# Sliding-window attention in a decoder layer: turned probabilities leave PSUM by a plain ScalarE copy, and the masked ones meet the difference of two neighbouring blocks' values

## The chip, the core and the metric

The kernel runs on one core of a Trainium2 chip. The metric is the device time of one execution in microseconds (us); the time before is 1079.05 us, the median of three runs from 1078.88 to 1079.31 us. The engines are named as in the profile: PE is TensorE (PEld its weight loads), ACT is ScalarE, DVE is VectorE, POOL is GpSimd, and SP issues most of the DMAs. A row of the trace gives the start in us from the beginning of the span, then the length, the engine, the source line, the operation and the tiles with their shapes.

## The reference, cut to what matters

One decoder layer is computed for 1024 prompt tokens and 8 x 4 sample tokens. Half of its mixing part is grouped-query attention with 8 query heads and 2 key/value heads of 64 elements, where each query sees itself and the 127 keys before it:

```python
d = a + WINDOW - c                       # query a of a block, key c of (block before, own block)
mask = (d >= 0)[None] & (d < WINDOW)[None] & (blk * WINDOW + c[None] - WINDOW >= 0)
...
m = jnp.maximum(jnp.max(s, axis=-1, keepdims=True), sink)
p = jnp.exp(s - m)
denom = jnp.sum(p, axis=-1, keepdims=True) + jnp.exp(sink - m)
w = (p / denom).astype(v.dtype)
return jnp.einsum('bnhgqk,bnkhd->bnqhgd', w, v)
```

A query at place a of a block (of 128 tokens) sees exactly 128 keys: those at places 0 to a of its own block and those at places a+1 to 127 of the block before. So one tile of 128 x 128 per head holds all its scores: column k belongs to the own block where k <= a and to the block before where k > a.

## The kernel before, in words

Features lie on the partitions and tokens on the free axis; the 1056 tokens are three groups of 352. All large products run on PE as three matmuls on split operands (high times high, high times low, low times high), 128x352 each. The program has one stage after another: the input projections (to about 129 us of the span), the attention (about 129 to 215 us) with the first output projections woven into it, and then the feed-forward and the per-layer input, which take the rest. `pinned` (from L572 on) keeps every instruction of PE in the order in which the program writes it. On the other engines a scheduler places the instructions, unless `tc.keep_in_program_order` (in `fix`, when `fixed[0]` is set, or directly) holds one to the written order; each engine then works through its list strictly in order.

The attention handles the eight blocks of 128 prompt tokens in the order 6, 7, 5, 0, 1, 2, 3, 4. `scores(b)` makes the scores of a block in PSUM; ACT copies four pieces of 128x256 out (L775), and DVE overwrites the columns that belong to the other half's keys (`copy_predicated`, L779). For block 0 DVE adds a mask instead (L781). `weigh(t)` is the softmax, once for each key/value head with 4 query heads: DVE takes the maximum (L721), the shift `nmx` (L723) and the sink's part `es` (L725); ACT does the exponentials (L729 for the sink, four at L732 with their sums); DVE adds and inverts the sums (L737, L738); POOL multiplies the tile by them (L740). `turned(b, t)` turns the eight 128x128 tiles on PE (L122), four into a PSUM bank; DVE takes them out twice, each time with a mask: `ptc` (L800) for the keys of the own block and `ptp` (L802) for the keys of the block before. `values(b, parts)` multiplies them by the values: in each half of the queries, `vmix` or `vtok` by `ptc`, and onto it the block before's `vtok` by `ptp`; `put` (L711 on ACT, L712 on DVE) stores the result split as high and low in `mixa`, which the output projection reads.

`filler(n)` puts n pieces of the output projection on PE between these steps: `out_pool` (12 matmuls; ACT copies the result out, L893), `out_attn` (12 matmuls that read `mixa`; DVE adds, L912, ACT squares and scales, L899, L902, L914) and `out_proj` (24 matmuls; ACT scales and squares, L922, L902). Weights come by SP's DMAs and are split by a cast of ACT (L173) and a subtraction of DVE (L174).

On PE the loop at L960 to L972 runs, for a block a and the next block b: scores(b), filler, the turning of a, filler, values(a). The first pass has no scores, since block 7's were made ahead.

Of the kernel before, what the change touches and what calls it, by code (L numbers as in the profile page):

```python
# [62 lines left out]
def trunk_kernel(  # L63
# [48 lines left out]
    def act_tile(shape, dt=F32, s="a"):  # L112
        return apool.tile(shape, dt, tag="a", bufs=A_SLOTS, name=nm(s))
# [18 lines left out]
    def bank():  # L132
        return psum.tile([P, 512], F32, tag="b", name=nm("b"))
# [33 lines left out]
    def fix(ins):  # L167

        if fixed[0]:
            tc.keep_in_program_order(ins)  # L170
# [493 lines left out]
    nc.scalar.dma_start(ps_o, pso)  # L664


    misc = act_tile([P, 6, P])
    qd, am, vdec = misc[:, 0, :], misc[:, 1:5, :], misc[: NDEC * DSEQ, 5, :]
    for c in range(4):
        ge.tensor_copy(  # L670
            qd.rearrange("p (g c e) -> p g c e", g=4, c=4)[:, :, c, :],
# [6 lines left out]
    ge.tensor_scalar(nskd, skd, -1.0, None, op0=ALU.mult)  # L678


    vtok, vmix = act_tile([P, NB, P]), act_tile([P, NB, P])

    def v_turned():
        for h in range(2):
            ps = bank()
            for i in range(4):
                b = 4 * h + i
                mt(ps[:, i * P : (i + 1) * P], vT[:, b * P : (b + 1) * P])
            v = ps.rearrange("p (b c) -> p b c", c=P)
            se.copy(vtok[:, 4 * h : 4 * h + 4, :], v)  # L690
            ge.tensor_copy(vmix[0:64, 4 * h : 4 * h + 4, :], vtok[0:64, 4 * h : 4 * h + 4, :])
        ge.tensor_copy(vmix[64:P, 1:NB, :], vtok[64:P, 0 : NB - 1, :])
        ps = bank()
        mt(ps[: NDEC * DSEQ, :P], vT[:, SEQ:])
        se.copy(vdec, ps[: NDEC * DSEQ, :P])
        nc.scalar.dma_start(kp_o, kT[:, SEQ - WIN : SEQ])
        nc.scalar.dma_start(vp_o, vtok[:, NB - 1, :])
# [17 lines left out]
    def softmax(*parts):  # L715

        scale = 0.125
        held = []
        for t, nh, sk, nsk in parts:
            mx = spool.tile([P, nh], F32, tag="mx", name=nm("mx"))  # L720
            fix(ve.tensor_reduce(mx, t, axis=AX.X, op=ALU.max))  # L721
            nmx = spool.tile([P, nh], F32, tag="nmx", name=nm("nmx"))
            fix(ve.scalar_tensor_tensor(nmx, mx, -scale, nsk, op0=ALU.mult, op1=ALU.min))  # L723
            es = spool.tile([P, nh], F32, tag="es", name=nm("es"))
            fix(ve.tensor_tensor(es, sk, nmx, op=ALU.add))  # L725
            held.append((nmx, es))
        sums = []
        for (t, nh, _, _), (nmx, es) in zip(parts, held):
            se.activation(es, es, AF.Exp)  # L729
            sm = spool.tile([P, nh], F32, tag="sm", name=nm("sm"))  # L730
            for c in range(nh):
                se.activation(  # L732
                    t[:, c, :], t[:, c, :], AF.Exp, bias=nmx[:, c : c + 1], scale=scale, accum_out=sm[:, c : c + 1]
                )
            sums.append(sm)
        for (t, nh, _, _), (_, es), sm in zip(parts, held, sums):
            fix(ve.tensor_tensor(sm, sm, es, op=ALU.add))  # L737
            fix(ve.reciprocal(sm, sm))  # L738
            nk = t.shape[2]
            ge.tensor_tensor(t, t, sm.unsqueeze(2).to_broadcast([P, nh, nk]), op=ALU.mult)  # L740
# [50 lines left out]
    def turned(b, t):  # L791

        ptc = act_tile([P, 8, WIN])
        ptp = act_tile([P, 8, WIN]) if b else None
        for kv in range(2):
            ps = bank()
            hs = slice(4 * kv, 4 * kv + 4)
            for c in range(4):
                mt(ps[:, c * P : (c + 1) * P], t[:, 4 * kv + c, :])
            fix(ve.tensor_tensor(ptc[:, hs, :], v4(ps), m4(2), op=ALU.mult))  # L800
            if b:
                fix(ve.tensor_tensor(ptp[:, hs, :], v4(ps), m4(3), op=ALU.mult))  # L802
        return ptc, ptp

    def values(b, parts):


        ptc, ptp = parts
        sides = [(kv, slice(64 * kv, 64 * kv + 64), slice(4 * kv, 4 * kv + 4)) for kv in range(2)]
        if not b:  # L810
            o = bank()
            for kv, cols, hs in sides:
                mm(o[cols, :], vtok[:, b, cols], ptc[:, hs, :], start=True, stop=True)
            put(o, 0, WIN)
            return
        q = [slice(0, 64), slice(64, P)]
        os_ = [bank() for _ in range(2)]
        for i, v in enumerate((vmix, vtok)):
            for kv, cols, hs in sides:
                mm(os_[i][cols, :256], v[:, b, cols], ptc[:, hs, q[i]], start=True, stop=False)  # L820
        for i in range(2):
            for kv, cols, hs in sides:
                mm(os_[i][cols, :256], vtok[q[i], b - 1, cols], ptp[q[i], hs, q[i]], start=False, stop=True)
        for i in range(2):
            put(os_[i], b * WIN + 64 * i, 64)

# [133 lines left out]
    for a, b in zip(order, order[1:] + [None]):  # L960

        fixed[0] = lazy[0] = b is None
        t2 = ahead or (None if b is None else scores(b))
        ahead = None
        filler(1)
        parts = turned(a, t)
        if b is None:
            lazy[0] = False
            weights(WOA[1][0], 1)
        filler(1)  # L970
        values(a, parts)
        t = t2  # L972
# [489 lines left out]
def _layout(i):  # L1462

    f = lambda a: np.asarray(a, dtype=np.float32) if not isinstance(a, np.ndarray) else a
    i = {k: f(v) for k, v in i.items()}
    tok = lambda a, s, c: np.concatenate([a.reshape(-1, c), s.reshape(-1, c)]).reshape(T, c // P, P).transpose(2, 1, 0)
    heads = np.concatenate([np.r_[64 * c : 64 * c + 64, 64 * (4 + c) : 64 * (4 + c) + 64] for c in range(4)])
    w_in = i["w_in"][0]
    w_in = w_in[:, np.r_[512:768, heads, 768:1280]]
    w_out = i["w_out"][0][np.r_[heads, 512:1024]]  # L1470
    tiles = lambda w: w.reshape(w.shape[0] // P, P, w.shape[1] // P, P).transpose(2, 1, 0, 3)
    wd = i["w_down"][0]
    gains = np.stack([i[n][0].reshape(KC, P).T for n in ("norm_mix_pre", "norm_mix_post", "norm_ffn_pre", "norm_ffn_post")], 1)
    sinks = i["attn_sinks"][0]
    q, c = np.arange(WIN)[:, None], np.arange(WIN)[None, :]
    masks = np.stack([1.0 * np.where(q < 64, c <= q, c > q), np.where(c <= q, 0.0, NEG), 1.0 * ((q <= c) | ((q >= 64) & (c < 64))), 1.0 * (q > c)], 1)
    r = np.arange(P)[:, None]
    ri, rj = (r % 8) // DSEQ, r % DSEQ
    rb = 2 * (r // 32) + ri
    ki, kw = np.arange(2 * WIN)[None, :] // WIN, np.arange(2 * WIN)[None, :] % WIN  # L1480
    nb, nj = np.arange(NDEC * DSEQ)[None, :] // DSEQ, np.arange(NDEC * DSEQ)[None, :] % DSEQ
    dmask = np.concatenate([(ri == ki) & (kw > rj), (rb == nb) & (nj <= rj)], 1)
    pfix = np.stack([np.maximum(w / (np.arange(16) + 1.0), 1.0) for w in PW])
    out = {
        "x": tok(i["x_prompt"], i["x_sample"], D),
        "p": tok(i["p_prompt"], i["p_sample"], PLE),
        "w_in": tiles(w_in),
        "w_out_a": w_out[:, :512].reshape(2, 4, P, 2, 256).transpose(0, 3, 2, 1, 4),
        "w_out_b": tiles(w_out[:, 512:]),
        "w_pool": i["w_pool"][0].transpose(1, 0, 2),  # L1490
        "w_gu": np.stack([tiles(i["w_gate"][0]), tiles(i["w_up"][0])], 1),
        "w_dn": wd[: SLAB * NSLAB * P].reshape(NSLAB, SLAB, P, 2, 2, 2, P).transpose(0, 4, 3, 2, 1, 5, 6).reshape(NSLAB, 2, 2, P, KC, P),
        "w_dl": wd[SLAB * NSLAB * P :].reshape(REST, P, 2, 512).transpose(2, 1, 0, 3),
        "w_pg": tiles(i["w_ple_gate"][0]),
        "w_ple": i["w_ple"][0].reshape(2, P, 4, 256).transpose(2, 1, 0, 3),
        "gains": gains,
        "pscale": i["pool_scale"][0].reshape(4, P).T,
        "sink_p": np.broadcast_to(sinks, (P, 8)),
        "sink_d": np.tile(np.repeat(sinks.reshape(2, 4).T, 8, axis=0), (4, 1)),
        "masks": masks.astype(np.float32),  # L1500
        "dmask": np.where(dmask, 0.0, NEG).astype(np.float32),
        "pfix": np.broadcast_to(pfix, (P, 4, 16)).astype(np.float32),
        "ck": i["cache_k"][0].reshape(NDEC, WIN, P).transpose(2, 0, 1),
        "cv": i["cache_v"][0].reshape(NDEC, WIN, P).transpose(1, 0, 2),
        "st": i["state_pool"][0].reshape(NDEC, PST, 4, P).transpose(3, 2, 0, 1),
    }
    return {k: np.ascontiguousarray(v) for k, v in out.items()}
# [29 lines left out]
```

## Time and profile before

| what | value |
| --- | --- |
| median of the runs (three) | 1079.05 us |
| the profiled execution's own time | 1080.58 us |
| its span, first to last instruction | 1078.8 us |
| PE busy | 1069.6 us, 99% |
| DVE busy | 874.7 us, 81% |
| ACT busy | 510.2 us, 47% |
| POOL busy | 281.3 us, 26% |
| mean granted clock of TensorE | 0.998 |

Durations below are those of the profiled execution. PE's rows overlap, since matmuls are pipelined: two 128x352 matmuls in a row begin about 0.16 us apart though each row is 0.32 us long. On ACT and DVE a row begins about 0.1 us before the row ahead of it ends when nothing is waited for.

### The profile page before, as it was taken

The page shows a single profiled execution, that of the slowest core. Times are in us where ns is not written, and L with a number is a line of the kernel's source. Part 1 is how long each engine was busy: PE and PEld are TensorE (multiplying, and loading weights), DVE is VectorE, ACT ScalarE, POOL GpSimd, SP SyncE. Part 2 cuts the span into 40 slices and gives each one's busy share as a digit, 9 for nine tenths or more (in the row PEclk, how much of TensorE's full clock was granted, in tenths as well). Part 3 has the DMA queues.
Part 4 walks back from the last instruction along what each step waited for, and adds up shares of the span by engine and source line. Part 5 has one row for each costly group of instructions (what it writes and reads, how often), then busy time and mean ns, then how long its engine had stood idle before and what let it go on. Part 6 is the DMA issues. An engine that isn't in the chain of part 4 may idle for free. (4 is left out here: it accounts for less than half of the span.)

```text
span 1078.8 us, 18189 instructions
## 1 busy us (share of the span) xinstructions
PE 1069.6 (99%) x7107; PEld 1053.0 (98%) x7107; DVE 874.7 (81%) x1303; ACT 510.2 (47%) x872; POOL 281.3 (26%) x211
## 2 busy tenths in 40 slices
PE   8999999999999999999999999999999999999998
PEld 8999988899999999999999999999999999999998
DVE  6876378886979957796598898898899998969983
ACT  7423277664555533445543343344344455545431
POOL 0063032200000023454454454444442000023200
PEclk9999999999999999999999999999999999999999
DMA  8121311544543432412212212213235556464361
GB/s 299 57 74 39 102 58 37 201 159 144 201 168 131 137 98 78 152 60 93 84 60 98 79 59 98 80 59 106 73 112 182 186 160 244 152 214 162 98 201 60
DMA packets 43575, 130.91 MB, mean 121 GB/s; under 512 B 5061, under 2 KB 15717, under 8 KB 43489
## 3 DMA queue, kind: packets, MB, share of 16 engines
q1 hardware_dynamic: 42160, 127.98, 35.0%
q10 hardware_dynamic: 1328, 1.77, 0.5%
q8 instruction: 56, 0.92, 0.4%
q14 instruction: 31, 0.25, 0.1%
HBM read 113.86 MB, written 15.87 MB: 120 GB/s over the span
## 5 line engine op out<-in xcount | busy, mean ns | idle before, releaser
L1108 POOL TENSOR_TENSOR wr<-wr,wr 128x512 f32<-128x512 f32 x108 | 174.9, 1634 | 476.8 <-DMA wr<-in_w_gu_dram 238.1
L173 ACT CAST wh<-wr 128x1024 fp32r<-128x1024 f32 (+1 forms) x138 | 142.1, 1031 | 162.8 <-PE b L128 98.7
L174 DVE TENSOR_TENSOR wl<-wr,wh 128x1024 fp32r<-128x1024 f32 (+1 forms) x138 | 171.0, 1241 | 42.0 <-ACT wh L173 26.3
L128 PE MATMUL b<-fh,wh 128*128 128x352 f32 x624 | 201.7, 323 | 0.8 <-DVE p L1135 0.8
L128 PE MATMUL b<-fh,wl 128*128 128x352 f32 x624 | 200.1, 321 | 0.0
L128 PE MATMUL b<-fl,wh 128*128 128x352 f32 x624 | 200.0, 320 | 0.0
L173 ACT CAST sh<-wr 128x1024 fp32r<-128x1024 f32 x72 | 75.7, 1052 | 141.3 <-POOL wr L1108 138.9
L128 PE MATMUL b<-fh,sh 128*128 128x352 f32 x416 | 134.3, 323 | 0.0
L128 PE MATMUL b<-fl,sh 128*128 128x352 f32 x416 | 133.2, 320 | 0.0
L128 PE MATMUL b<-fh,sl 128*128 128x352 f32 x416 | 133.2, 320 | 0.0
L174 DVE TENSOR_TENSOR sl<-wr,sh 128x1024 fp32r<-128x1024 f32 x72 | 97.4, 1353 | 37.4 <-ACT sh L173 24.5
L128 PEld LDWEIGHTS b<-fh,wh 128*128 128x128 f32 x624 | 117.0, 187 | 1.5 <-DVE p L1135 1.1
L128 PEld LDWEIGHTS b<-fl,wh 128*128 128x128 f32 x624 | 117.5, 188 | 0.0
L128 PEld LDWEIGHTS b<-fh,wl 128*128 128x128 f32 x624 | 116.9, 187 | 0.0
L128 PE MATMUL b<-h,wh 128*128 128x352 f32 x480 | 105.9, 326 | 1.2 <-ACT h L449 1.1
L128 PE MATMUL b<-hid,wh 128*128 128x352 f32 x416 | 99.6, 322 | 0.0
L128 PEld LDWEIGHTS b<-h,wh 128*128 128x128 f32 x480 | 82.4, 190 | 2.5 <-ACT h L449 1.2
L1108 POOL TENSOR_TENSOR wr<-wr 128x512 f32<-128x512 f32 x36 | 50.9, 1414 | 106.7 <-DVE w L174 106.7
L128 PEld LDWEIGHTS b<-fl,sh 128*128 128x128 f32 x416 | 78.2, 188 | 0.0
L128 PEld LDWEIGHTS b<-fh,sh 128*128 128x128 f32 x416 | 78.0, 187 | 0.1
L128 PEld LDWEIGHTS b<-fh,sl 128*128 128x128 f32 x416 | 77.9, 187 | 0.0
L128 PE MATMUL b<-hp,sh 128*128 128x352 f32 x320 | 76.6, 322 | 0.9 <-DVE ap L1278 0.9
(202 smaller groups left out, 2220.7 us busy)
## 6 DMA issues: line engine op xcount, KB each, us to landing
wr<-in_w_gu_dram SPq DMA_DIRECT2D x88, 512.0 KB, 3.3
wr<-in_w_dn_dram SPq DMA_DIRECT2D x40, 512.0 KB, 3.3
wr<-in_w_pg_dram SPq DMA_DIRECT2D x16, 512.0 KB, 3.6
x<-in_x_dram SPq DMA_DIRECT2D x6, 704.0 KB, 8.6
x1d<-x SPq DMA_DIRECT2D x6, 704.0 KB, 3.6
x<-x1d SPq DMA_DIRECT2D x6, 704.0 KB, 5.1
out_y_dram<-yo SPq DMA_DIRECT2D x24, 176.0 KB, 2.3
wr<-in_w_out_b_dram SPq DMA_DIRECT2D x8, 512.0 KB, 3.3
```

The costliest lines, as they stand in the source:

```text
L128: ins = te.matmul(*args, **kw)
L173: fix(se.copy(hi, src))
L174: fix(ve.tensor_tensor(lo, src, hi.bitcast(F32), op=ALU.subtract))
L1108: ge.tensor_tensor(out, a, b, op=op)
```

## The change

The masked copy `ptc` becomes an unmasked one. On the 64 keys where a half of the queries meets both blocks, with p the turned probabilities, M their part that belongs to the block before, and v and v' the values of the own block and of the block before, the product was (p - M) v + M v', and is now p v + M (v' - v). So ACT copies the whole turned bank out, DVE makes only the masked `ptp`, and `ptp` meets `vdif`, the difference of two neighbouring blocks' values, which POOL makes once. The mask of the own block is gone from the tensor `masks` (four tiles before, three now). Two things move with it: the exponentials and the new copies on ACT are held in the written order, and the softmax of the next block is now written behind the turning of the present one.

```diff
-    misc = act_tile([P, 6, P])
-    qd, am, vdec = misc[:, 0, :], misc[:, 1:5, :], misc[: NDEC * DSEQ, 5, :]
+    misc = act_tile([P, 5, P])
+    qd, am, vdec = misc[:, 0, :], misc[:, 1:4, :], misc[: NDEC * DSEQ, 4, :]
...
-    vtok, vmix = act_tile([P, NB, P]), act_tile([P, NB, P])
+    vtok, vmix, vdif = (act_tile([P, NB, P]) for _ in range(3))
...
         ge.tensor_copy(vmix[64:P, 1:NB, :], vtok[64:P, 0 : NB - 1, :])
+        ge.tensor_tensor(vdif[:, 1:NB, :], vtok[:, 0 : NB - 1, :], vtok[:, 1:NB, :], op=ALU.subtract)
...
             for c in range(nh):
-                se.activation(
-                    t[:, c, :], t[:, c, :], AF.Exp, bias=nmx[:, c : c + 1], scale=scale, accum_out=sm[:, c : c + 1]
+                tc.keep_in_program_order(
+                    se.activation(
+                        t[:, c, :], t[:, c, :], AF.Exp, bias=nmx[:, c : c + 1], scale=scale, accum_out=sm[:, c : c + 1]
+                    )
                 )
...
-            fix(ve.tensor_tensor(ptc[:, hs, :], v4(ps), m4(2), op=ALU.mult))
+            tc.keep_in_program_order(se.copy(ptc[:, hs, :], v4(ps)))
             if b:
-                fix(ve.tensor_tensor(ptp[:, hs, :], v4(ps), m4(3), op=ALU.mult))
+                fix(ve.tensor_tensor(ptp[:, hs, :], v4(ps), m4(2), op=ALU.mult))
...
-                mm(os_[i][cols, :256], vtok[q[i], b - 1, cols], ptp[q[i], hs, q[i]], start=False, stop=True)
+                mm(os_[i][cols, :256], vdif[q[i], b, cols], ptp[q[i], hs, q[i]], start=False, stop=True)
...
-        t2 = ahead or (None if b is None else scores(b))
-        ahead = None
+        t2 = ahead or (None if b is None else scores(b, False))
         filler(1)
         parts = turned(a, t)
+        if t2 and not ahead:
+            weigh(t2)
+        ahead = None
```

The lines of the changed kernel lie a little lower: the new copy is L803 and the remaining masked product L805; L732 is L734 there, L729 is L730, L723 and L725 are L724 and L726, L711 and L712 are L712 and L713, L893 is L896, L902, L914 and L922 are L905, L917 and L925, L775 and L779 are L778 and L782, and `vdif` is L693. The order of PE's instructions is the same in both; what moves stands on ACT and DVE, at three places.

The first place is ACT's list around the values of block 6, the first block. Here `a_1497` (before) and `a_1499` (now) is the tile of block 7, whose scores were made ahead, `y` is the result of a piece of the output projection, and `a_1608` is the `ptc` of block 6. Before:

```order
L711 CAST mh_1582<-b_1427 128x4x32
L732 ACTIVATE a_1497,sm_1541<-a_1497,nmx_1536 128x128
L729 ACTIVATE es_1538<-es_1538 128x4
L732 ACTIVATE a_1497,sm_1541<-a_1497,nmx_1536 128x128 x3
L729 ACTIVATE es_1553<-es_1553 128x4
L732 ACTIVATE a_1497,sm_1556<-a_1497,nmx_1551 128x128 x4
L957 DMA out_ks_dram<-a_1586 128x1024
L893 COPY y_1285<-b_1592 128x352
```

And now:

```order
L712 CAST mh_1584<-b_1429 128x4x32
L896 COPY y_1285<-b_1594 128x352
L730 ACTIVATE es_1540<-es_1540 128x4
L734 ACTIVATE a_1499,sm_1543<-a_1499,nmx_1538 128x128 x4
L730 ACTIVATE es_1555<-es_1555 128x4
L734 ACTIVATE a_1499,sm_1558<-a_1499,nmx_1553 128x128 x4
L960 DMA out_ks_dram<-a_1588 128x1024
L803 COPY a_1608<-b_1610 128x512
L803 COPY a_1608<-b_1617 128x512
```

The copy of `y`, which waits for a filler on PE, stood behind the eight exponentials of block 7 and stands ahead of them now, and the two copies that the values of block 6 need stand behind all of these.

The second place is DVE's list where block 0's scores (`a_1775`, now `a_1777`) meet block 5's turned tiles. The waits are printed with the rows of the change. Before:

```order
L723 SCALAR_TENSOR_TENSOR nmx_1790<-mx_1788,c_1289 128x4
L723 SCALAR_TENSOR_TENSOR nmx_1805<-mx_1803,c_1289 128x4
L800 TENSOR_TENSOR a_1832<-b_1834,a_1280 128x512
L725 TENSOR_TENSOR es_1792<-c_75,nmx_1790 128x4
L725 TENSOR_TENSOR es_1807<-c_75,nmx_1805 128x4
```

And now:

```order
L805 TENSOR_TENSOR a_1805<-b_1806,a_1280 128x512 [waits Activation_49]
L805 TENSOR_TENSOR a_1805<-b_1813,a_1280 128x512 [waits Activation_49]
L726 TENSOR_TENSOR es_1824<-c_75,nmx_1822 128x4 [waits DVE_49]
L724 SCALAR_TENSOR_TENSOR nmx_1837<-mx_1835,c_1289 128x4
L726 TENSOR_TENSOR es_1839<-c_75,nmx_1837 128x4 [waits DVE_49]
```

Both masked products now stand ahead of `es`, and each waits for ACT, that is for the copy out of the same bank. On ACT the sink's exponential, which reads `es`, now comes ahead of the four others of its head, where one to three of them came first before.

The third place is ACT's list in one of the later rounds of the loop, from block 3's scores (`a_2173`, now `a_2175`) to its exponentials; `a_2236` is the `ptc` of block 2, and `sq` and `y` belong to the fillers. Before:

```order
L775 COPY a_2173<-b_2175 128x256
L775 COPY a_2173<-b_2177 128x256
L732 ACTIVATE a_2173,sm_2217<-a_2173,nmx_2212 128x128 x2
L729 ACTIVATE es_2214<-es_2214 128x4
L732 ACTIVATE a_2173,sm_2217<-a_2173,nmx_2212 128x128 x2
L729 ACTIVATE es_2229<-es_2229 128x4
L732 ACTIVATE a_2173,sm_2232<-a_2173,nmx_2227 128x128 x4
L902 ACTIVATE sq_2260<-y_1287 128x352
L914 ACTIVATE y_1287<-y_1287,c_72 128x352
```

And now:

```order
L173 CAST wh_2282<-wr_2216 128x1024
L778 COPY a_2175<-b_2177 128x256
L778 COPY a_2175<-b_2179 128x256
L905 ACTIVATE sq_2232<-y_1287 128x352
L917 ACTIVATE y_1287<-y_1287,c_72 128x352
L803 COPY a_2236<-b_2238 128x512
L803 COPY a_2236<-b_2245 128x512
L730 ACTIVATE es_2256<-es_2256 128x4
L734 ACTIVATE a_2175,sm_2259<-a_2175,nmx_2254 128x128 x4
L730 ACTIVATE es_2271<-es_2271 128x4
L734 ACTIVATE a_2175,sm_2274<-a_2175,nmx_2269 128x128 x4
```

The exponentials stood right behind the copies of the scores; now the square and the scaling of a filler's result and the two new copies stand between, and a weight cast has come in among the copies of the scores.

More of the change, by code (lines that the diff above doesn't have):

```diff
@@ L1475, in _layout @@
     q, c = np.arange(WIN)[:, None], np.arange(WIN)[None, :]
-    masks = np.stack([1.0 * np.where(q < 64, c <= q, c > q), np.where(c <= q, 0.0, NEG), 1.0 * ((q <= c) | ((q >= 64) & (c < 64))), 1.0 * (q > c)], 1)
+    masks = np.stack([1.0 * np.where(q < 64, c <= q, c > q), np.where(c <= q, 0.0, NEG), 1.0 * (q > c)], 1)
     r = np.arange(P)[:, None]
```

## The prediction

> **What bounds the kernel now.** I read the page's busy times first, then what PE waited for, then the attention by stretches, and then the rows around three places of the loop. The page's first part gives busy time, share and instructions by engine:
>
> ```profile
> PE 1069.6 (99%) x7107; PEld 1053.0 (98%) x7107; DVE 874.7 (81%) x1303; ACT 510.2 (47%) x872; POOL 281.3 (26%) x211
> ```
>
> PE is busy for 99% of the span, so only its waits can be won, and every new wait is lost in full. The list of waits of PE (line, releaser, us in total, times, longest) has one entry that this change touches:
>
> ```profile
> PE b L128 <- DVE a L800: 0.5, 1, 0.5
> ```
>
> It is the wait for a masked copy that the change removes, 0.5 us. PE's order and work don't change, so about 0.5 us bounds the gain; 0.2% of this kernel, about what a measurement can tell from no change, is 2.2 us. The stretches of the attention's later rounds (PE, PEld, DVE, ACT, POOL busy, clock, DMA):
>
> ```profile
> 180.00:190.90 10.90, 10.90 (x117) 9.94 (x116) 10.74 (x24) 8.78 (x31) 2.34 (x2) 1.00 0.29 98
> 190.90:200.00 9.10, 8.57 (x98) 6.99 (x95) 8.07 (x24) 5.53 (x24) 2.20 (x2) 1.00 0.19 60
> ```
>
> ACT is no spare engine here: of 10.9 us in the first it is busy for 8.78.
>
> **What is removed and added.** The groups (count, then busy time and mean ns) over the attention:
>
> ```profile
> L800 DVE TENSOR_TENSOR a<-b,a 128x512 f32<-128x512 f32 x16 | 10.9, 682 | 1.6 <-PE b L122 1.5
> L802 DVE TENSOR_TENSOR a<-b,a 128x512 f32<-128x512 f32 x14 | 9.4, 675 | 0.0
> L893 ACT COPY y<-b 128x352 f32<-128x352 f32 x12 | 5.2, 442 | 5.3 <-PE b L128 5.2
> L690 ACT COPY a<-b 128x512 f32<-128x512 f32 x2 | 1.1, 588 | 7.3 <-PE b L122 7.3
> ```
>
> DVE loses the 16 of L800, 10.9 us. ACT gains 16 copies of the kind of L690, 16 x 0.59 = 9.4 us, two for each block. The 14 of L802 stay, but each now waits for the copy out of its bank. `vdif` is one POOL product of 128x896; by L740's row of 128x576 below (1.15 us) it takes about 1.15 x 896/576 = 1.8 us, and it fits in POOL's idle time between these two rows, from 132.2 to 135.5:
>
> ```profile
> 131.29 0.93 POOL L692 COPY a<-a 64x896 f32<-64x896 f32 x1
> 135.53 1.15 POOL L740 TENSOR_TENSOR a<-a,sm 128x576 f32<-128x576 f32 x1 [3.31 <-ACT a L775]
> ```
>
> It and the smaller mask cost nothing there; without that cover they would delay block 6's softmax, which has until 147.74. What counts is the order on ACT: 9.4 us more of work that waits for PE's turning, with exponentials, casts and PSUM copies queued behind it. The softmax that is written later takes its maxima, its exponentials, its sums and POOL's two products with it, so PE's next turning gets them later. Three places follow; primes mark times on before's clock, without the waits added earlier.
>
> **First place, the values of block 6: +1.9 us.** The rows of PE and ACT (start, length):
>
> ```profile
> 147.58 0.32 PE L128 MATMUL b<-mh,wl 128*128 128x352 f32 x1
> 147.74 1.04 PE L122 MATMUL b<-c,a 128*128 128x128 f32 x8
> ...
> 150.61 3.01 PE L128 MATMUL b<-a,a 128*64 128x256 f32 x64
> ```
>
> ```profile
> 146.95 0.40 ACT L732 ACTIVATE a<-a,nmx 128x128 f32<-128x128 f32 x1 [0.87 <-DVE nmx L723]
> ...
> 150.24 0.94 ACT L893 COPY y<-b 128x352 f32<-128x352 f32 x2
> ```
>
> Before, block 7's exponentials ran from 146.95 to 150.24, 3.29 us, beside the filler, and `y` was copied behind them. Now `y` comes first. Its filler's last matmul ends at 147.9 (147.58 + 0.32); the copy takes 0.44, and the exponentials begin at 148.3 and end their turn at 151.6. Only then come the copies of block 6: 0.59, and 1.1 for both, so they end at 152.2 and 152.7. PE wants the first at 150.61: it waits 1.6 us there, then 0.2 for the second, since a first product of 0.26 us lies between, and at most 0.1 for the products of DVE (0.68 behind each copy). Sum 1.9. From below: 1.2, if `y` and the exponentials run somewhat closer than the rows; from above 2.3, if each of the four hand-overs costs 0.1 more.
>
> **Second place, the filler that reads block 5's result: +1.4 us.** The rows on DVE, ACT and PE:
>
> ```profile
> 160.28 1.00 DVE L737 TENSOR_TENSOR sm<-sm,es 128x4 f32<-128x4 f32 x1
> 161.31 0.18 DVE L738 RECIPROCAL sm<-sm 128x4 f32<-128x4 f32 x1
> 161.41 0.72 DVE L712 TENSOR_TENSOR ml<-b,mh 128x256 fp32r<-128x256 f32 x2
> 162.05 1.28 DVE L781 TENSOR_TENSOR a<-b,a 128x512 f32<-128x512 f32 x2
> 163.25 1.27 DVE L721 TENSOR_REDUCE mx<-a 128x4 f32<-128x512 f32 x2
> 164.43 0.28 DVE L723 SCALAR_TENSOR_TENSOR nmx<-mx,c 128x4 f32<-128x4 f32 x2
> ```
>
> ```profile
> 155.61 1.05 ACT L173 CAST wh<-wr 128x1024 fp32r<-128x1024 f32 x1 [1.29 <-PE b L128]
> ...
> 164.67 0.40 ACT L732 ACTIVATE a<-a,nmx 128x128 f32<-128x128 f32 x1 [0.84 <-DVE nmx L723]
> ...
> 167.96 0.43 ACT L893 COPY y<-b 128x352 f32<-128x352 f32 x1
> 168.44 0.65 ACT L711 CAST mh<-b 128x256 fp32r<-128x256 f32 x2
> ```
>
> ```profile
> 169.65 0.43 PE L128 MATMUL b<-mh,wh 128*128 128x352 f32 x1
> ```
>
> Before, `put` ended on ACT at 169.09 (168.44 + 0.65) and the filler began at 169.65: next to no slack. Now block 5's exponentials follow the cast, `y` and the copies of block 7: 156.6 + 0.4 + 1.0 = 158.0', and end at 161.3'. Their sum and its inverse then end at about 161.7', where they ended at 161.5 before (161.31 + 0.18), since the sum's row was held for 1.00 us. With `put` behind `y`, block 0's scores follow at 162.6' instead of 162.05: +0.5. The two maxima and `nmx` move with them, and then both L805 stand ahead of `es`: 2 x 0.64 + 0.15 (as long as one `nmx`), so ACT begins at 166.5' where it began at 164.67: +1.8. Exponentials (3.29), `y` (0.4) and both casts (0.65) end at 170.8', 1.1 us after 169.65; the low part on DVE, half of 0.72, adds 0.3. Sum 1.4. Its ends are 0, if the scheduler's rows overlap as well as before, and 2.0, if the new sum is held on DVE as the old one was, for 1.00 us.
>
> **Third place, the rounds of blocks 2 to 4: +2.6 us.** PE's values begin here:
>
> ```profile
> 185.93 3.01 PE L128 MATMUL b<-a,a 128*64 128x256 f32 x64
> ...
> 195.98 0.65 PE L128 MATMUL b<-a,a 128*64 128x256 f32 x2
> 197.11 3.01 PE L128 MATMUL b<-a,a 128*64 128x256 f32 x62 [0.48 <-DVE a L800]
> ...
> 206.88 1.68 PE L128 MATMUL b<-a,a 128*64 128x256 f32 x16
> ```
>
> So PE's rounds take 10.05 and 10.90 us, the second with the old wait in it. Now ACT and DVE form a closed ring per round, by the new order:
>
> ```profile
> 189.51 1.22 ACT L775 COPY a<-b 128x256 f32<-128x256 f32 x4
> ...
> 197.73 0.48 ACT L902 ACTIVATE sq<-y 128x352 f32<-128x352 f32 x1
> 198.24 0.59 ACT L914 ACTIVATE y<-y,c 128x352 f32<-128x352 f32 x1
> 198.74 0.54 ACT L922 ACTIVATE y<-b,c 128x352 f32<-128x352 f32 x1
> 199.17 0.45 ACT L902 ACTIVATE sq<-b 128x352 f32<-128x352 f32 x1
> ```
>
> ```profile
> 178.46 1.23 DVE L174 TENSOR_TENSOR wl<-wr,wh 128x1024 fp32r<-128x1024 f32 x1 [0.26 <-ACT wh L173]
> ...
> 191.67 1.43 DVE L779 COPY_PREDICATED a<-a,b 128x256 f32<-128x256 int32 x4
> ...
> 194.25 0.51 DVE L912 TENSOR_TENSOR y<-y,b 128x352 f32<-128x352 f32 x1
> ```
>
> First score copy 0.4, predicated copies 1.43, `y` 0.51, square and scaling 0.48 + 0.51, then copy and two L805 0.59 + 1.28, `es` 0.15, exponentials 3.29, the filler's scaling and square 0.78 (from 198.74 to 0.1 before the square's end at 199.62), both casts of `put` 0.5: 9.9 us. Six hand-overs between ACT and DVE of 0.05 make it 10.2. A weight split stands in each ring: in block 2's the subtraction is ahead of the predicated copies (+1.0 of its 1.23), in block 3's cast and subtraction stand in their middle (+1.9). So the rings take 11.2 and 12.1 against 10.05 and 10.90: +1.15 and +1.2. What ACT is late on entry, less the slack of POOL's product before the turning, I take as +0.3. Sum 2.6, which comes due at the values of block 2, a filler or two and the last turning. The low end is 0.4 (the splits find other room), the high end 4.5 (each split takes 1.8 us and more, as one row that ran beside POOL's product did):
>
> ```profile
> 186.17 1.80 DVE L174 TENSOR_TENSOR wl<-wr,wh 128x1024 fp32r<-128x1024 f32 x1
> ```
>
> [...]
>
> **Sum.** 1.9 + 1.4 + 2.6 = 5.9 us. The profiled execution took 1080.58 us by itself (span 1078.8), 1.5 above the median of the runs; with the change that is 1086.5, and on the median 1079.05 + 5.9 = 1085.0 us. The low ends give 1.6, 1080.7 us; the high ends 8.8, 1087.9 us.
>
> **Rivals.** (1) Not slower: the copies hide. ACT is busy for 47% of the whole span, and DVE, the busier engine (10.74 of 10.9 us above), loses 10.9 us; the old wait of 0.5 goes: 1079.05 - 0.5 = 1078.5 us. It decides at block 6's values: if they wait under 0.3 us for ACT, the copies are hidden. Against it: the order puts `y` and all exponentials ahead of them. Chance 0.09. (2) Only the first place holds, and the later ones are absorbed by DVE's shorter queue: 1079.05 + 1.9 = 1081.0 us, within the 0.2%. Chance 0.09. (3) The rings grow further: POOL's product slows DVE's splits (1.80 against 1.23) and holds its sums (1.00, where L738's row has 0.18), about 0.6 + 0.8 per round, twice: 1085.0 + 2.8 = 1087.8 us. Chance 0.16. (4) PE's idling lowers its clock. The clock was below full only in the first stretch, where it lost 0.09 x 20 = 1.8 us:
>
> ```profile
> 0.00:20.00 20.00, 17.16 (x87) 16.13 (x88) 11.60 (x21) 14.89 (x26) 2.11 (x17) 0.91 0.95 324
> ```
>
> One such loss gives 1085.0 + 1.8 = 1086.8 us. Against it: each of the new waits is under 2 us and PE works between them. Chance 0.04. [...] (5) The forecast: 0.62.
>
> **How the numbers follow.** The time is the forecast's, 1085.0 us. The range goes from 1080.6 (low ends, rival 2) to 1088.6 us (the high ends and rival 3); it leaves out rival 1 and the tails. Slower by over 0.2%, above 1081.2 us, are the forecast, rivals 3 and 4 and part of 2: 0.83. Within 0.2% are most of rivals 1 and 2: 0.14. Faster by over 0.2% would need more than PE's one wait: 0.03.
>
> **What would show it.** In the new profile PE should wait some 1.6 us for L803 at block 6's values near 150.6, about 1 us for `mh` (L712, L713) near 172, and less than a us each near block 2's values and at the turning of block 4 (for POOL's L743); DVE's busy time should be about 11 us less and ACT's 9 more, and everything from 225 us on should be the same but later. It is wrong if PE has no wait for L803 over 0.3 us, if the exponentials are not ahead of the copies, or if the loss comes from elsewhere, such as after the attention.

## The result and the profile after

The changed kernel takes 1087.97 us (median of six runs, 1085.57 to 1088.86) where the kernel before, run beside it, takes 1079.53: a ratio of 1.0079, 95% interval 1.0068 to 1.0089, or 8.4 us more. Two later comparisons give 1.0064 (1.0050 to 1.0078) and 1.0066 (1.0053 to 1.0078), 7.3 and 6.8 us. The change is slower, within the range, by 1 to 2.5 us more than the forecast. The first profiled execution took 1088.1 us, its span 1086.0.

Busy times of the changed kernel, then its list of PE's waits:

```profile
PE 1072.8 (99%) x7107; PEld 1055.3 (97%) x7107; DVE 868.1 (80%) x1287; ACT 517.7 (48%) x888; POOL 281.6 (26%) x212
```

```profile
PE b L128 <- ACT a L803: 1.8, 2, 1.5
PE b L128 <- ACT mh L712: 1.7, 1, 1.7
PE b L431 <- POOL c L156: 1.6, 1, 1.6
PE b L122 <- POOL a L743: 1.2, 2, 1.0
PE b L122 <- DVE ml L713: 1.0, 1, 1.0
```

DVE lost 6.6 us and ACT gained 7.5; before's one wait in the attention is gone, and four of these five entries are new (each gives the total, the number of waits and the longest; L431's also stood before, with the same 1.6 us). The groups of the added and kept instructions:

```profile
L805 DVE TENSOR_TENSOR a<-b,a 128x512 f32<-128x512 f32 x14 | 9.0, 681 | 0.0
L803 ACT COPY a<-b 128x512 f32<-128x512 f32 x16 | 8.6, 582 | 0.3 <-PE b L122 0.3
L693 POOL TENSOR_TENSOR a<-a 128x896 f32<-128x896 f32 x1 | 2.1, 2112 | 0.1
```

**First place.** ACT and PE at the values of block 6:

```profile
147.50 0.45 ACT L896 COPY y<-b 128x352 f32<-128x352 f32 x1 [1.86 <-PE b L128]
147.85 0.21 ACT L730 ACTIVATE es<-es 128x4 f32<-128x4 f32 x1
...
150.74 0.39 ACT L734 ACTIVATE a<-a,nmx 128x128 f32<-128x128 f32 x1
151.13 1.05 ACT L803 COPY a<-b 128x512 f32<-128x512 f32 x2
...
151.75 1.56 PE L128 MATMUL b<-a,a 128*64 128x256 f32 x8 [1.50 <-ACT a L803]
```

The copy of `y` goes first, eight exponentials follow, the two copies come last, and PE waits for the first of them: the order of the lists, in time.

**Second place.** DVE, ACT and PE before the filler that reads block 5's result:

```profile
166.61 1.28 DVE L805 TENSOR_TENSOR a<-b,a 128x512 f32<-128x512 f32 x2
167.81 0.15 DVE L726 TENSOR_TENSOR es<-c,nmx 128x4 f32<-128x4 f32 x1
```

```profile
168.05 0.21 ACT L730 ACTIVATE es<-es 128x4 f32<-128x4 f32 x1 [1.57 <-DVE nmx L724]
...
171.34 0.43 ACT L896 COPY y<-b 128x352 f32<-128x352 f32 x1
171.67 0.63 ACT L712 CAST mh<-b 128x256 fp32r<-128x256 f32 x2
```

```profile
172.35 0.43 PE L128 MATMUL b<-mh,wh 128*128 128x352 f32 x1 [1.67 <-ACT mh L712]
```

ACT stood idle for 1.57 us until `es` and the `nmx` right behind it were there, both behind the two masked products. Behind PE's wait for `mh` something else happened. The records of PE's granted clock begin in this trace at 10.00, 173.84, 177.25 and 1085.20 us (1.00, 0.50, 1.00 and 0.50), which lie 48, 1 and 266 times 3.413 us apart. The stretches on this grid around the two long waits (PE, PEld, DVE, ACT, POOL busy, clock, DMA):

```profile
149.95:153.36 3.41, 1.91 (x14) 0.80 (x17) 1.74 (x5) 2.57 (x11) 2.08 (x2) 1.00 0.39 156
170.43:173.84 3.41, 1.65 (x19) 1.26 (x11) 2.12 (x8) 2.94 (x13) 2.08 (x2) 1.00 0.00 0
173.84:177.25 3.41, 3.41 (x16) 3.34 (x15) 2.36 (x9) 0.99 (x5) 0.00 (x0) 0.50 0.00 0
```

For 3.41 us PE ran at half clock, and fell 1.5 us further behind.

**Third place.** POOL, DVE and PE at the turning of block 3, and DVE's first sum of blocks 1, 2 and 3:

```profile
206.10 1.04 POOL L743 TENSOR_TENSOR a<-a,sm 128x512 f32<-128x512 f32 x1 [0.57 <-DVE sm L741]
206.30 1.22 DVE L906 TENSOR_TENSOR acc<-acc,sq 128x352 f32<-128x352 f32 x1 [0.34 <-ACT sq L905]
206.41 0.63 PE L122 MATMUL b<-c,a 128*128 128x128 f32 x4
207.45 0.61 DVE L713 TENSOR_TENSOR ml<-b,mh 128x256 fp32r<-128x256 f32 x2
208.00 0.63 PE L122 MATMUL b<-c,a 128*128 128x128 f32 x4 [0.96 <-DVE ml L713]
```

```profile
179.94 0.16 DVE L740 TENSOR_TENSOR sm<-sm,es 128x4 f32<-128x4 f32 x1 [3.37 <-ACT a L734]
...
191.91 0.16 DVE L740 TENSOR_TENSOR sm<-sm,es 128x4 f32<-128x4 f32 x1 [0.60 <-ACT a L734]
...
203.94 0.16 DVE L740 TENSOR_TENSOR sm<-sm,es 128x4 f32<-128x4 f32 x1 [1.61 <-ACT a L734]
```

The rings of ACT and DVE take 11.97 and 12.03 us. The second half of block 3's turning waits for the bank from which `put`'s low part (L713) is still read.

**The account.** PE does the same instructions in the same order in all these kernels, so the start of the same matmul in two traces, one less the other, is how far one is behind. The table gives by how much that lag grows (us) in stretches named by before's clock; extra matmuls of an experiment are left out of the count. The last column is the median of the runs less that of before beside it (for the move alone, one of whose five executions took 3751 us and is left out, its ratio times before's 1079.06, less that).

| kernel | to block 6's values (130–155) | to the filler (155–168.5) | its start (168.5–170.2) | behind it (170.2–178) | rounds (178–225) | sum | runs |
| --- | --- | --- | --- | --- | --- | --- | --- |
| changed | 2.04 | -0.63 | 2.10 | 1.50 | 2.75 | 7.8 | +8.4 |
| changed, again | 2.05 | -0.63 | 2.30 | 1.24 | 3.44 | 8.4 | +7.3 |
| changed, third time | 2.05 | -0.64 | 2.11 | 1.49 | 2.70 | 7.7 | +6.8 |
| the move alone | 0 | 0.15 | 2.41 | 1.49 | 4.53 | 8.6 | +7.6 |
| the copy on ACT, softmax unmoved | 1.08 | 4.32 | 0 | 1.10 | 6.30 | 12.8 | +12.2 |
| the same, order free | 1.08 | 4.36 | 0 | 0.97 | 2.80 | 9.2 | +9.4 |
| moved, copy on DVE | 0 | 0.15 | 2.41 | -0.11 | 3.64 | 6.1 | +6.5 |
| block 7's softmax late | -0.01 | -0.63 | 2.10 | -0.13 | 3.85 | 5.2 | +5.3 |
| seven extra matmuls | 2.06 | -0.64 | 3.02 | 0.37 | 2.57 | 7.4 | +7.7 |
| four extra matmuls | 2.07 | -0.64 | 2.15 | 0.12 | 4.30 | 8.0 | +7.0 |
| shifts first | 0 | -0.64 | 1.52 | -0.13 | 2.48 | 3.2 | +3.5 |
| vdif alone | 0 | 0.04 | 0 | 0 | 0 | 0 | -0.5 |
| plain copies first | 0 | -0.34 | 0.13 | 0.16 | 1.55 | 1.5 | +1.4 |

From 225 us on no kernel's lag grows by more than 0.4 us (the changed kernel's by 0.3); in most traces it shrinks, by up to 2.9 us, since before's profiled execution, 1.5 us above the first median, had waits there (`p` at L1135, `ap` at L1278) that are shorter or absent in the others. So the account of the attention is read, not the spans.

### The profile page after: what moved, and what is told of

It reads as the page before. It is cut to its first block, busy times and chain, and to the rows that moved or that the text cites. A ratio compares the mean times of both kernels' runs of the same rounds, so it can differ in the third digit from the quotient of the medians.

```text
span 1086.0 us, 18183 instructions
## 1 busy us (share of the span) xinstructions
PE 1072.8 (99%) x7107; PEld 1055.3 (97%) x7107; DVE 868.1 (80%) x1287; ACT 517.7 (48%) x888; POOL 281.6 (26%) x212
## 5 line engine op out<-in xcount | busy, mean ns | idle before, releaser
L174 DVE TENSOR_TENSOR wl<-wr,wh 128x1024 fp32r<-128x1024 f32 (+1 forms) x138 | 168.8, 1226 | 42.9 <-ACT wh L173 27.9
L174 DVE TENSOR_TENSOR sl<-wr,sh 128x1024 fp32r<-128x1024 f32 x72 | 97.2, 1350 | 37.7 <-ACT sh L173 24.7
```

Of the source, the lines that this page charges most:

```text
L174: fix(ve.tensor_tensor(lo, src, hi.bitcast(F32), op=ALU.subtract))
```

## The experiments

**The move alone**: the kernel before, with the softmax behind the turning and its exponentials held; both masked copies stay on DVE. The edit against the kernel before, cut:

```diff
-                se.activation(
...
+                tc.keep_in_program_order(
+                    se.activation(
...
-        t2 = ahead or (None if b is None else scores(b))
-        ahead = None
+        t2 = ahead or (None if b is None else scores(b, False))
...
+        if t2 and not ahead:
+            weigh(t2)
+        ahead = None
```

> The kernel before with only the move: the softmax of the next block is written behind the turning, its exponentials are held in the written order, and DVE still makes both masked copies (the product with vdif is absent, ACT has no new copies). Theory, the place of the softmax makes the loss and the copies only add to it at block 6's values: DVE now has four masked products (2.6 us) ahead of the sink's part where the changed kernel has one copy and two products (1.9 us), so the second place and the rounds of blocks 2 to 4 lose at least as much as in the changed kernel, block 6's values lose nothing; 1084 to 1089 us. Rival, the added ACT copies themselves are the price (ACT is the engine that waits): without them little is left, 1079 to 1081 us.

The ratio is 1.0070 (1.0056 to 1.0084), 7.6 us over before's 1079.06. Without any new copy on ACT the second place and the rounds lose as much as in the changed kernel or more, and the half clock is there too; block 6's values lose nothing. PE's waits:

```profile
PE b L122 <- POOL a L742: 5.2, 7, 1.0
PE b L128 <- ACT mh L711: 1.9, 1, 1.9
```

The rival falls: the later place of the softmax is enough for the later losses.

**The copy without the move**: the ACT copies stay held, the softmax goes back into the making of the scores, and its exponentials are free again, as before. The edits from here on are cuts against the changed kernel, where nothing else is said.

```diff
-        t2 = ahead or (None if b is None else scores(b, False))
+        t2 = ahead or (None if b is None else scores(b))
...
-        if t2 and not ahead:
-            weigh(t2)
```

> The changed kernel with the move taken back: the softmax is written inside the making of the scores as before, its exponentials are free again, the ACT copies (held in the written order) and vdif stay. Theory, the place of the softmax makes the loss: at block 6's values the copies still stand behind the exponentials and y, about 1 us; the rounds of blocks 2 to 4 are as before, no half clock; 1080 to 1082 us. Rival, ACT's 16 added copies are the price wherever the softmax stands: 1085 us and more.

1091.22 us, 1.0119 (1.0103 to 1.0134): my theory missed by 9 us. Its list of waits, then ACT and PE at the values of block 1:

```profile
PE b L128 <- ACT a L801: 9.8, 7, 2.9
```

```profile
194.41 1.04 ACT L801 COPY a<-b 128x512 f32<-128x512 f32 x2
...
195.02 1.60 PE L128 MATMUL b<-a,a 128*64 128x256 f32 x5 [2.92 <-ACT a L801]
```

With the softmax in its old place the exponentials of the next block stand ahead of the copies in every round, as they do at the first place of the changed kernel in only one, and each round's values wait. So each costs by itself, the place without the copies and the copies without the move: ACT has one list, and either the copies or the exponentials are late.

**The plain copy on DVE**: as the changed kernel, but for one engine.

```diff
-            tc.keep_in_program_order(se.copy(ptc[:, hs, :], v4(ps)))
+            tc.keep_in_program_order(ve.tensor_copy(ptc[:, hs, :], v4(ps)))
```

> The changed kernel, but the plain copy out of the turned bank is made by DVE, not ACT; vdif and the move stay. Theory: at block 6's values DVE isn't behind the exponentials, so that wait of 1.9 us goes; at the second place and in the rounds DVE has a copy and a product for each bank ahead of the sink's part (2.6 us in place of 1.9), so the later losses of about 6.5 us (waits and half clock) stay or grow by 1 to 2; 1084 to 1088 us. Rival, ACT's added copies are the price: 1079 to 1081 us.

1085.51 us, 1.0060 (1.0048 to 1.0073). The first place is gone, as expected, and the rounds lose 3.64. But PE waited even longer for the filler, and the half clock was not there; the filler's first matmul and three stretches on this trace's grid:

```profile
171.33 0.43 PE L128 MATMUL b<-mh,wh 128*128 128x352 f32 x1 [1.91 <-ACT mh L712]
```

```profile
166.99:170.40 3.41, 2.43 (x62) 1.78 (x58) 0.92 (x6) 3.02 (x17) 0.63 (x1) 1.00 0.02 5
170.40:173.82 3.42, 2.32 (x13) 2.06 (x14) 2.90 (x9) 1.95 (x8) 1.45 (x2) 1.00 0.00 0
173.82:177.23 3.41, 3.41 (x25) 3.41 (x24) 2.69 (x8) 1.83 (x6) 0.00 (x0) 1.00 0.00 0
```

The 1.91 us fall on both sides of a border, about 1.0 and 1.1 in each window, and the clock stays at 1.00.

**The wait filled**: matmuls into the bank of the filler's first matmul, ahead of it.

```diff
+        if (m, g) == (0, 2):
+            for _ in range(7):
+                mm(ps[:, : 2 * P], ones, vtok[:, 0:2, :], start=True, stop=True)
```

> The changed kernel with seven extra matmuls of 128x256 on PE, put into the bank of the filler out_attn(0,2) ahead of its own first matmul, which clears the bank: 7 x about 0.12 us or more of work in a stretch in which PE waits 1.9 us for mixa (the extra work changes no result). Theory, the 1.6 us that PE loses right behind this wait are a half clock that the wait itself brings: with the wait filled the clock stays full, PE's later matmuls 0.16 us apart, and the time is 1.6 us less than the changed kernel's, 1085.5 to 1087. Rival, the half clock comes from something else (the wait at block 6's values, a fixed moment): half clock stays, same time as the changed kernel or up to 1 us more, 1087.5 to 1089.

1086.75 us, 1.0073 (1.0060 to 1.0085): the half clock is gone, but the seven take 2.93 us (171.38 to 174.31), 0.42 each, so PE begins the filler 0.9 us later, and the rounds lose 2.57; 0.7 us less than the changed kernel by the difference to before, which is too little to tell, and not the theory's 1.6.

**The changed kernel again.**

> The changed kernel once more, for a second profile and as the measure of the runs beside it. Theory, PE's clock is judged over windows of 3.41 us whose phase differs from run to run, and it is halved for the next window when PE idled for more than about half of one (drops so far behind windows with 1.76, 2.07 and 2.47 us of idling, none behind 1.50): the same waits as in the first profile within 0.3 us, the half clock behind the filler's wait only if most of that 1.7 us falls into one window, and single times spread over 1.6 us, 1086 to 1089. Rival, the half clock belongs to the place: it comes again at the same matmul, and with it the same time.

1085.75 us, 1.0064 (1.0050 to 1.0078), with the half clock behind the same wait again; the third profile below has it too. The profiles speak for neither side by themselves, but the mean clock of each execution is on record: 3.41 us at half clock take it to 0.998 or below, and six of the sixteen executions of the changed kernel have 1.000. So the half clock doesn't come in every run, and the rival falls.

**Block 7's softmax behind block 6's turning**, beside the last.

```diff
-    ahead = scores(order[1])
+    ahead = scores(order[1], False)
...
-        if t2 and not ahead:
+        if t2:
             weigh(t2)
```

> The changed kernel, but the softmax of block 7 too is written behind the turning of block 6, as all later ones are. Theory, the first place is the queue of ACT: the copies of block 6 now stand ahead of block 7's exponentials, PE's wait for them at block 6's values (2.0 us in the profile) goes, block 7 has 13 us until its turning and isn't late; 2.0 us less than the changed kernel, 1085 to 1087. Rival, the copies or vdif themselves are late (vdif's 2.1 us on POOL, the copy's own time): the wait stays, 1087 to 1089.

1083.82 us, 1.0044 (1.0031 to 1.0057), 1.9 us less than the changed kernel beside it: the copies themselves cost nothing at the first place, their standing behind block 7's exponentials does. The filler's wait is the same 1.67 us as there, and the clock stays full, the wait lying across a border:

```profile
166.73:170.14 3.41, 1.95 (x58) 1.69 (x56) 0.76 (x5) 3.41 (x18) 1.13 (x2) 1.00 0.02 5
170.14:173.55 3.41, 3.11 (x21) 2.85 (x21) 3.41 (x9) 1.23 (x5) 0.95 (x1) 1.00 0.00 0
```

**Shifts first**: besides that, maxima, `nmx` and `es` (now made by `shifts`) are written ahead of the turning.

```diff
+        held = [shifts(p) for p in parts_of(t2)] if t2 else None
         parts = turned(a, t)
-        if t2 and not ahead:
-            weigh(t2)
+        if t2:
+            weigh(t2, held)
```

> The run before this one, and besides the maxima, nmx and es of the next block are written ahead of the turning, only the exponentials, the sums and POOL's product behind it; so on DVE es stands ahead of one or both masked products. Theory, the later losses are the ring of ACT and DVE (copy, masked products, es, exponentials, product, turning): up to 1.3 us less in each round, so the second place and the rounds lose 2 to 4 us less than before, and the half clock may go; 1081 to 1085 us. Rival, ACT's load by itself (copies and exponentials of one round, whatever DVE does) sets the rounds: as the run before this one, 1085 to 1087.

1081.97 us, 1.0031 (1.0020 to 1.0041): 1.9 us less again, 0.6 of it at the filler and 1.4 in the rounds by the account. With fewer products of DVE ahead of `es` the ring is shorter, so DVE's order is part of the cost.

**vdif and the mask alone**: the plain copy on DVE, the softmax unmoved and free.

```diff
-            tc.keep_in_program_order(se.copy(ptc[:, hs, :], v4(ps)))
+            fix(ve.tensor_copy(ptc[:, hs, :], v4(ps)))
...
-        t2 = ahead or (None if b is None else scores(b, False))
+        t2 = ahead or (None if b is None else scores(b))
```

> The kernel before with vdif and the one mask alone: DVE makes the unmasked copy by itself, the softmax stays where it was, nothing is held. Theory, vdif, the mask and the other right operand of PE cost nothing: 1079 to 1080 us, as the kernel before. Rival, the product of 128x896 on POOL delays the first softmaxes or slows DVE: 1080.5 to 1082 us.

1077.95 us, 0.9990 (0.9981 to 0.9999). In the attention it is before to 0.04 us, so `vdif`, the mask and the other operand cost nothing. So the 0.5 us by the runs can only lie behind the attention, and they are below what can be told; I don't claim a gain.

**Four extra matmuls**, beside the changed kernel for the third time; the edit is against the run with seven.

```diff
-            for _ in range(7):
+            for _ in range(4):
```

> The changed kernel a third time, as the measure of the run with the short fill beside it, and for a third phase of the clock's windows. If the filler's wait of 1.7 us falls across the border of two windows, the clock stays full and PE's 1.5 us of slow matmuls are missing, but the rounds of blocks 2 to 4, whose ring on ACT and DVE doesn't depend on PE's clock, then lose 3.4 to 3.9 us where they lost 2.75 in the first profile; 1085.5 to 1088 us either way. Rival, the half clock comes at this place in every run, whatever the phase.

> As the run with seven extra matmuls, but with four, about 0.42 us each in that run, so that PE is busy through the filler's wait and isn't delayed beyond it. Theory, the half clock costs less than it shows: it goes, the matmuls behind the filler run at 0.16 us apart, but the rounds of blocks 2 to 4 wait for the ring of ACT and DVE instead, 3.4 to 3.9 us; over the attention 0.4 to 1.2 us less than the changed kernel, not 1.5. Rival, all of the half clock's loss comes back: 1.5 us less than the changed kernel beside it, and rounds that lose 2.75 as in the first profile.

1085.92 us (1.0066, 1.0053 to 1.0078) for the changed kernel, whose rival falls as the one before did, and 1086.12 (1.0068, 1.0054 to 1.0082) with the fill. The windows of the fill, then its turning of block 2:

```profile
170.26:173.67 3.41, 3.36 (x55) 2.70 (x46) 1.45 (x7) 3.41 (x17) 1.82 (x2) 1.00 0.02 5
173.67:177.08 3.41, 3.37 (x23) 3.35 (x24) 3.32 (x11) 1.09 (x7) 0.26 (x1) 1.00 0.00 0
```

```profile
195.87 0.63 PE L122 MATMUL b<-c,a 128*128 128x128 f32 x4
197.45 0.63 PE L122 MATMUL b<-c,a 128*128 128x128 f32 x4 [0.96 <-DVE ml L713]
```

The half clock is gone and nothing is won. By the account PE enters the rounds 1.3 us less late (2.07 - 0.64 + 2.15 + 0.12 = 3.70 us against 5.01), and waits there 1.6 us more (4.30 against 2.70): block 2's turning now waits too. Neither my theory's 0.4 to 1.2 us nor the rival's 1.5 came. But this run changes more than the clock. With the fill the scheduler gave ACT and DVE another order behind it: the cast and the split of a weight moved ahead, and the split (L174, at 182.73) took 1.77 us beside POOL's product where the changed kernel's took 1.21. With seven the order differs as well. So the two fills by themselves don't show what the half clock costs. The executions of the changed kernel do, since their program is the same and their mean clock differs: those at 1.000 took 1088.04 us in the first set, 1086.15, 1085.54 and 1085.75 in the second, 1086.10 and 1085.06 in the third, and the others 1085.57 to 1088.86, 1085.51 to 1085.79 and 1085.48 to 1086.12. No gain of the full clock can be told.

**The copy on ACT, unmoved and free**, beside these: the copy without the move, and its ACT copies no longer held.

```diff
-            tc.keep_in_program_order(se.copy(ptc[:, hs, :], v4(ps)))
+            fix(se.copy(ptc[:, hs, :], v4(ps)))
```

> The changed kernel with the move taken back and the new copies free too, so that the scheduler may put them ahead of the next block's exponentials; it does so in the later rounds only. Theory, on ACT a copy either stands behind the exponentials (then the values wait for it) or delays them (then the next turning and put wait): at blocks 6, 7 and 5 the same 5 us as with the copies held, in the rounds of blocks 1 to 4 less than the 6 us lost there; 1084 to 1089 us. Rival, holding the order alone makes the loss: 1079 to 1081 us.

1088.57 us, 1.0091 (1.0077 to 1.0105): the same 5.4 us up to the filler, 2.8 in the rounds in place of 6.3 (which have a half clock in them, shown at the end). Holding the order is not the cause; a free order only finds some of the better places. With the runs above this closes a square: the plain copy on DVE costs 0.04 us in the attention with the softmax in its old place and 6.1 behind the turning; on ACT it costs 9.2 or 12.8, and 7.8.

**Plain copies first**, beside these, from the kernel with `vdif` alone.

```diff
+        both = []
...
             fix(ve.tensor_copy(ptc[:, hs, :], v4(ps)))
-            if b:
-                fix(ve.tensor_tensor(ptp[:, hs, :], v4(ps), m4(2), op=ALU.mult))
+            both.append((hs, ps))
+        for hs, ps in both:
+            if b:
+                fix(ve.tensor_tensor(ptp[:, hs, :], v4(ps), m4(2), op=ALU.mult))
```

> The kernel with vdif and the one mask alone, with both plain copies of DVE written ahead of both masked products, since PE's values want the second plain copy 0.5 us after the first and the masked ones only behind four products. Theory, the two places of before where the values of blocks 7 and 2 stand 0.64 us apart too far are the wait for the second plain copy behind the first masked one: both go, 1.3 us less than that kernel, 1076 to 1077.5 us where that kernel and before are at 1078 to 1079. Rival, what ends there is the softmax's sum and its inverse, which stand between on DVE: no change.

1080.54 us, 1.0013 (1.0005 to 1.0022), slower than before by 1.4 us. The two places, which are the values of blocks 5 and 2, gave 0.34 and 0.33 us, not 0.64 each, and the scheduler put a group of DVE behind the last filler's addition (L916, L912 of before) where it stood ahead of it, and PE waited for it:

```profile
222.93 0.52 DVE L916 TENSOR_TENSOR y<-y,b 128x352 f32<-128x352 f32 x1 [1.39 <-PE b L128]
...
223.77 0.95 DVE L402 TENSOR_TENSOR dg<-c,dg 128x352 fp32r<-128x352 f32 x2
...
224.34 0.86 PE L128 MATMUL b<-dg,c 128*128 128x352 f32 x2 [1.45 <-DVE dg L402]
```

No version here is shown to beat before.

## Why the prediction was right, and where it was off

- **What bounds the kernel** held: the new waits of PE are what the time grew by, and 16 products (10.9 us) fewer on DVE bought nothing. That PE's one old wait of 0.5 us bounds the gain was too narrow: at the values of blocks 5 and 2 the lag shrank by 0.64 each.
- **What is added**: 0.58 us a copy against 0.59, 2.1 us for `vdif` against 1.8, hidden as said (`vdif` alone costs 0.04). DVE's busy time fell by 6.6 us, not 11: the additions told of below took 2.6 us more, and the rest is spread over other rows. ACT's rose by 7.5, not 9.
- **First place**: 1.9 forecast, 2.04 to 2.05 in the three profiles, and gone when block 7's softmax was written later. Rival 1 falls with it.
- **Second place**: 1.4 forecast. Its start loses 2.10, of which 0.63 is the old wait's end ahead of it: 1.47. The mechanism was shown when `es` came earlier: 0.6 less. Rival 2 falls here.
- **What would show it**: the waits for L803 (1.5 against 1.6) and for `mh` (1.7 against 1), and POOL's at the turning of block 4, stand where they were forecast. The wait of 0.96 for L713's bank at block 3's turning was not foreseen.
- **Third place**, the term that was mis-sized: 2.6 forecast. It reads 2.70 to 3.44 in the three profiles, but there PE comes late to the rounds by a half clock as well. With the clock full, and with the same order on ACT and DVE in the rounds, it is 3.85 (block 7's softmax late). The ring of block 2 was put at 11.2 us and took 11.97 (11.95 with the clock full), block 3's at 12.1 and took 12.03 (12.04). What the sum lacked in the first is, by the rows, the price of POOL beside DVE: the addition of squares (L906) takes 1.22 us beside POOL's product, as the rows at 206 show. Three rows of before:

```profile
187.96 0.51 DVE L903 TENSOR_TENSOR acc<-acc,sq 128x352 f32<-128x352 f32 x1
188.58 0.53 DVE L903 TENSOR_TENSOR acc<-acc,sq 128x352 f32<-128x352 f32 x1
188.71 1.30 POOL L740 TENSOR_TENSOR a<-a,sm 128x512 f32<-128x512 f32 x1 [1.82 <-DVE sm L738]
```

  The first addition has no product of POOL beside it. The second began ahead of one, and it was the product that took longer, 1.30 us in place of 1.04. In the attention of before's trace and of the changed kernel's first it goes by the order of starting: the seven additions that began behind the start of a product of POOL ended 0.37 to 0.39 us behind the product's end (0.61 to 1.22 us long), the others took 0.49 to 0.53. In the changed kernel it begins 0.20 us behind POOL, in each of these rounds, and it stands ahead of L713 and of the next scores' predicated copies on DVE. Rival 3 had this mechanism at the weight splits, which kept their 1.21 or 1.22 us; at the additions it came true, for about 0.7 us a round, and the result lies between the forecast's 5.9 us and this rival's 8.7. That the addition makes the difference is read from rows and not shown: no run took POOL's product away, and with the plain copy on DVE the seven additions took 0.62 us on the mean, where the changed kernel's took 0.92, while the rounds lost 3.64, most of it through other rows.
- **Rival 4**, given 0.04: the clock did fall, to 0.50 behind a wait of 1.67 us, so what was held against it, waits under 2 us with PE at work between them, failed. (Before's stretch from 190.9 to 200, with a wait of 0.48 us, had 1.00.) But its price was wrong too. On PE it is 1.5 us, and in the time it is nothing that these runs can show: executions of the changed kernel at full clock took as long as the others. In the run with block 7's softmax late, PE comes to the rounds less late by the half clock's 1.6 us (-0.13 against 1.50), and 1.1 of it goes into longer waits there (3.85 against 2.75). So the half clock isn't why the result lies above the forecast; the rounds are.
- **The masked product behind the copy**: L805 began at 151.72 where the first L803 ended at 151.13 + 0.58 = 151.71. That is a hand-over of 0.01 us by these rows; the 0.05 in the sum was an estimate. The dependency is in the program, as the waits in DVE's list show; no run with the copy on ACT left it out, so what L805 beside the copy would take stays open.

## What to carry to other kernels

An engine that is busy for half the span can still be full where it counts (ACT before: 47% of the span, but 8.78 of 10.9 us in one stretch of the rounds): ask which instructions stand ahead of a moved one on its new engine, and which now stand behind it. Where two engines pass each other results in a closed ring, work out the ring's time: here rings of 11.97 and 12.03 us, where PE's rounds took 10.05 and 10.90 before, made PE wait, and of the 1.6 us that PE lost ahead of them to its half clock, 1.1 ended as less waiting there. An instruction put in to fill a wait can also change what the scheduler does with other engines, so compare the order of their rows before reading the result. Compare traces by the same matmul's start, stretch by stretch, since spans hold waits elsewhere that come and go.

## What the runs showed of the hardware

In these traces PE's clock changes on a grid of 3.41 us (the changed kernel's four times are given above), at phases that differ from run to run: the halved window begins at 173.84 us in the changed kernel's first profile, at 174.04 in its third and at 172.94 in the move alone, less than a window apart. A window that was only partly idle was enough: the clock was halved after windows in which PE worked 1.65 or 1.66 of 3.41 us (the first and the third profile of the changed kernel) and, in two other traces, less:

```profile
169.52:172.94 3.42, 1.35 (x18) 0.97 (x9) 1.95 (x9) 3.28 (x16) 2.08 (x2) 1.00 0.00 0
172.94:176.35 3.41, 3.41 (x15) 3.34 (x14) 2.09 (x7) 0.24 (x1) 0.00 (x0) 0.50 0.00 0
```

```profile
191.16:194.57 3.41, 0.94 (x6) 0.65 (x5) 1.67 (x6) 3.41 (x13) 2.26 (x2) 1.00 0.47 156
194.57:197.98 3.41, 2.96 (x16) 1.49 (x20) 2.68 (x4) 1.68 (x4) 0.00 (x0) 0.50 0.38 135
```

The first pair is the move alone, the second the held copy without the move. It was not halved after 1.91 (changed kernel at 149.95) and 1.95 (block 7's softmax late), and a wait of 1.91 us across a border, with 2.43 and 2.32 us of work in its two windows, passed (the plain copy on DVE). So in the attention the halvings read came behind 1.66 us of work and less, and none came behind 1.91 and more. Elsewhere the two overlap: in the start of before's trace the clock was halved behind a window with 2.16 us of work.

```profile
4.54:7.95 3.41, 2.16 (x10) 1.30 (x10) 2.52 (x5) 2.50 (x5) 0.00 (x0) 1.00 1.03 334
7.95:11.37 3.42, 3.42 (x13) 3.25 (x13) 2.35 (x5) 2.08 (x5) 0.00 (x0) 0.50 1.04 375
```
